# Leaky-ReLU matmul on one core: the first two regions take shorter turns in k, and only the first run of A is turned by TensorE

## The chip, the cores and the metric

One core of a Trainium2 chip runs the kernel. The metric is the device time of one execution in microseconds. Several executions are taken of each kernel, and those of the kernel before are taken on the same chip in the same rounds.

## The reference

```python
def setup_inputs():
    m, k, n = 4096, 4096, 4096
    # a: (m, k) float32 normal, b: (k, n) float32 normal, alpha = 0.01
def reference(a, b, alpha):
    x = np.matmul(a, b)
    return np.where(x > 0, x, alpha * x)
```

## The kernel before

The output is cut into regions of 512 rows by 1024 columns. A region fills all of PSUM: 4 row tiles (`mt`) times 2 column halves (`nt`) are 8 banks. k comes in four units (`u`) of 1024, each of 8 chunks (`c`) of 128. A has to lie with k on the partitions. The usual way there is "strips": GpSimd sends DMAs that cast to bfloat16 and lay four strips of k on four groups of 32 partitions, and VectorE's 32x32 stream transpose (`turn`) does the rest. B comes by casting DMAs of one chunk each.

The first two regions are special, since nothing is there yet. The first unit of A and B comes over the hardware DMA queue as float32 and is cast on chip; A is then transposed by TensorE into PSUM and copied out. The two regions take turns, and what PSUM holds at the end of a turn goes to an SBUF tile `part` (a copy the first time, an add after).

```python
RUNS = [2, 1, 1, 1]                # unit 0 is laid out in two runs of 512 in k
TURNS = [[0], [1], [2, 3]]         # both regions do unit 0, then unit 1, then units 2 and 3
...
order = [("b", 0), ("a", 0, 0, 1), ("a", 1, 0, 1), ("a", 2, 0, 1), ("a", 3, 0, 1)]
order += [("b", 1), ("b", 2), ("a", 0, 1, 2), ("b", 3), ("a", 2, 1, 1), ("a", 3, 1, 1)]
order += [("b", c) for c in range(4, KC)]        # hardware loads, 6 MB in all
...
        if (what, i) == ("b", 3):                # GpSimd's DMAs start behind this copy
            nc.gpsimd.tensor_copy(x[:, :1], b0[:, 3, :1])
...
    turns[1][0](0, 1)                            # transpose the first strips of region 1
    for mt in range(MT):
        spill(0, 0, mt, banks)                   # bank (mt,0) by ScalarE, (mt,1) by VectorE
        if mt == 0:
            turns[1][0](1, 2)
```

## Time and profile before

| what | us | where from |
|---|---|---|
| time, median of 3 | 1783.36 (1783.19 to 1783.38) | runs |
| span of the profiled run | 1781.5 | page |
| lost before and between matmuls | 10.28 | worked out at the top of the prediction |

The one number to watch is the lost time: the end of the last matmul less the 1768.1 us that the matmuls need without a break. I call "stop" a gap between two matmul starts over the normal 216 ns. Some later traces lack 163 of the 8224 matmul records, which shows as single gaps of just two distances (about 432 ns); these are not stops and are left out.

### The profile page before, as it was taken

How to read it: one execution, taken by the hardware profiler on the slowest of the kernel's cores; microseconds unless marked ns; L12 is line 12 of the kernel's file. 1: busy time of each engine (PE TensorE's matmuls, PEld its weight loads, DVE VectorE, ACT ScalarE, POOL GpSimd, SP SyncE). 2: the span in 40 equal slices, each digit the busy share in tenths (PEclk: the TensorE clock that was granted, in tenths of full speed). 3: DMA queues.
4: the chain of work that ended last, by engine and by line, in shares of the span. 5: the costliest groups of instructions: out<-in, count | busy, mean ns of one | idle time of the engine just before them, and what ended most of it. 6: DMA issues, size and time to landing. Idle time of an engine off the chain costs nothing.

```text
span 1781.5 us, 18212 instructions
## 1 busy us (share of the span) xinstructions
PE 1775.6 (100%) x8267; PEld 807.6 (45%) x8267; DVE 144.9 (8%) x123; ACT 152.5 (9%) x271; POOL 366.1 (21%) x667
## 2 busy tenths in 40 slices
PE   9999999999999999999999999999999999999999
PEld 4444444444444444444444444444444444444444
DVE  4530000032000000002200000000220000000000
ACT  2010000000000000000000000000000000000001
POOL 5630200433002020144201202014320110301000
PEclk9999999999999999999999999999999999999999
DMA  9995653988039164398704817449860481835511
GB/s 250 199 251 119 117 128 88 190 130 124 36 95 189 48 121 116 95 192 134 124 24 97 187 48 144 93 105 196 134 122 13 112 172 48 163 73 120 116 48 47
DMA packets 161548, 214.06 MB, mean 120 GB/s; under 512 B 41536, under 2 KB 90816, under 8 KB 161472
## 3 DMA queue, kind: packets, MB, share of 16 engines
q0 software_dynamic: 140608, 139.50, 49.4%
q10 hardware_dynamic: 18432, 67.12, 9.7%
q1 hardware_dynamic: 2432, 6.29, 0.9%
q8 instruction: 64, 1.05, 0.2%
q14 instruction: 12, 0.10, 0.0%
HBM read 285.21 MB, written 67.11 MB: 198 GB/s over the span
## 4 chain that ended last, share of the span: by engine, by line
PE 99%; DMA 0%; ACT 0%; DVE 0%; SPq 0%; issue 0%
PE ps L160 99%; DMA a_in<-in_a_dram 0%; PE turned L290 0%; DVE at L297 0%; ACT at L297 0%; ACT bt L301 0%; DVE a_rounded L273 0%; ACT o L444 0%; SPq L263 0%
## 5 line engine op out<-in xcount | busy, mean ns | idle before, releaser
L160 PE MATMUL ps<-bt,at 128*128 128x512 bf16 x8224 | 1769.8, 378 | 0.5 <-ACT at L297 0.2
L160 PEld LDWEIGHTS <-at 128*128 128x128 bf16 x8224 | 804.2, 98 | 964.1 <-issue 1.4
L140 POOL DMA_DIRECT2D bt<-in_b_dram x408 | 217.1, 538 | 1084.8 <-PE ps L160 1035.8
L429 ACT ACTIVATE o<-ps 128x512 f32<-128x512 f32 x239 | 130.2, 595 | 1518.2 <-PE ps L160 1442.0
L123 DVE STREAM_TRANSPOSE at<-a 128x1024 uint32<-128x1024 uint32 (+2 forms) x64 | 112.5, 1793 | 1154.4 <-DMA a<-in_a_dram 937.9
L117 POOL DMA_DIRECT2D a<-in_a_dram x252 | 148.2, 595 | 194.9 <-DVE at L123 132.4
L238 DVE TENSOR_TENSOR part<-ps,part 128x512 f32<-128x512 f32 x32 | 20.2, 686 | 25.0 <-PE ps L160 25.0
L241 ACT ACTIVATE o<-part 128x1024 f32<-128x1024 f32 x8 | 8.5, 1057 | 77.0 <-DVE part L238 63.4
L301 ACT CAST bt<-b_in 128x512 bf16<-128x512 f32 x8 | 4.9, 619 | 9.6 <-DMA b_in<-in_b_dram 9.6
L234 DVE COPY part<-ps 128x512 f32<-128x512 f32 x8 | 5.3, 681 | 4.0 <-PE ps L160 4.0
L236 ACT COPY part<-ps 128x512 f32<-128x512 f32 x8 | 4.4, 593 | 13.6 <-issue 8.1
L89 PE MATMUL wp<-w 128*128 128x512 bf16 x11 | 4.0, 532 | 1.2 <-DVE x L80 1.2
L290 PE MATMUL turned<-ident,a_rounded 128*128 128x128 bf16 x32 | 2.9, 222 | 1.0 <-DVE a_rounded L273 1.0
L301 DVE CAST bt<-b_in 128x512 bf16<-128x512 f32 x8 | 3.5, 440 | 4.1 <-DMA b_in<-in_b_dram 4.1
L273 DVE CAST a_rounded<-a_in 128x512 bf16<-128x512 f32 (+1 forms) x7 | 3.2, 469 | 5.7 <-DMA a_in<-in_a_dram 5.6
L290 PEld LDWEIGHTS <-a_rounded 128*128 128x128 bf16 x32 | 2.2, 115 | 3.0 <-DVE a_rounded L273 2.7
L89 PEld LDWEIGHTS <-w 128*128 128x128 bf16 x11 | 1.3, 127 | 3.4 <-issue 1.9
L350 POOL CAST x<-bt 128x1 f32<-128x1 bf16 x1 | 0.2, 183 | 12.1 <-ACT bt L301 12.1
L297 ACT COPY at<-turned 128x512 bf16<-128x512 bf16 x4 | 2.3, 586 | 0.7 <-PE turned L290 0.5
L297 DVE COPY at<-turned 128x1024 bf16<-128x1024 bf16 x2 | 1.4, 692 | 1.2 <-PE turned L290 1.2
L86 ACT ACT_TABLE_LOAD x1 | 1.3, 1283 | 1.2 <-PEq L463 1.2
L444 ACT ACTIVATE o<-ps 128x256 f32<-128x256 f32 x2 | 0.8, 384 | 6.0 <-PE ps L160 6.0
(9 smaller groups left out, 1.4 us busy)
## 6 DMA issues: line engine op xcount, KB each, us to landing
bt<-in_b_dram POOLq DMA_DIRECT2D x408, 256.0 KB, 8.0
out_dram<-o ACTq DMA_DIRECT2D x127, 512.0 KB, 3.3
a<-in_a_dram POOLq DMA_DIRECT2D x244, 128.0 KB, 5.3
b_in<-in_b_dram SPq DMA_DIRECT2D x7, 512.0 KB, 8.5
a_in<-in_a_dram SPq DMA_DIRECT2D x6, 256.0 KB, 5.2
b_in<-in_b_dram ACTq DMA_DIRECT2D x1, 512.0 KB, 4.7
a_in<-in_a_dram SPq DMA_DIRECT2D x1, 512.0 KB, 7.6
a<-in_a_dram POOLq DMA_DIRECT2D x8, 64.0 KB, 5.3
```

The costliest lines, as they stand in the source:

```text
L89: nc.tensor.matmul(wp, w[:, :P], w, start=True, stop=True)
L117: nc.gpsimd.dma_start(to, src.rearrange("(g i) w -> i g w", i=32))
L123: nc.vector.transpose(dst.rearrange("p c m e -> p c (m e)").bitcast(U32) .rearrange("p c (g i) -> p g c i", i=32), held[0][:, 4 * t0:4 * t ...
L140: nc.gpsimd.dma_start(new_b(pi, u)[:, c, :], b_rows(n, u, c))
L160: nc.tensor.matmul(ps, plain(t)[:, c, rows] if (mb, h, u) == (0, 0, 0) else t[:, c // 2, rows, c % 2], bt[pi, u][:, c, cols or slice(nt * ...
L234: nc.vector.tensor_copy(kept, banks[mt, nt])
L236: nc.scalar.copy(kept, banks[mt, nt])
L238: nc.vector.tensor_add(kept, banks[mt, nt], kept)
L241: nc.scalar.activation(o, part[h][:, mt, :], LRELU, alpha=alpha)
L290: nc.tensor.transpose(turned[:, c, slot, :], cols[:, i + t, c, :], ident)
L301: copy(b0[:, i, columns(nt)], b_in[i][:, columns(nt)])
L429: nc.scalar.activation(o[:, cols], banks[mt, nt], LRELU, alpha=alpha)
```

## The change

The intent: TensorE's second batch of transposes sits in its stream before 16 us. If region 0 starts with 512 of k only, and region 1 takes over, the second run of A can come as strips instead. It then needs a finer set of turns (512, 512, 512, 1536, 2048, 2048, 1024 of k), and half of the hardware loads move to GpSimd's queue.

```diff
-RUNS = [2, 1, 1, 1]
+SEGS = [(0, 0, 4), (0, 4, 4), (1, 0, 8), (2, 0, 8), (3, 0, 8)]     # unit, first chunk, chunks
-TURNS = [[0], [1], [2, 3]]
+TURNS = [(0, [0]), (1, [0]), (0, [1]), (1, [1, 2]), (0, [2, 3]), (1, [3, 4]), (0, [4])]
+WHERE = {1: [4, 4, 4, 4], 2: [2, 2, 4, 4], 4: [3, 5, 5, 5]}        # where transposes go
...
-order = [("b", 0), ("a", 0, 0, 1), ...                              # 15 hardware loads
+order = [("b", 0)] + [("a", mt) for mt in range(MT)] + [("b", c) for c in range(1, kc0)]   # 8
...
-        if (what, i) == ("b", 3):
-            nc.gpsimd.tensor_copy(x[:, :1], b0[:, 3, :1])
+        if (what, i) == ("a", MT - 1):
+            nc.gpsimd.tensor_copy(x[:, :1], a_rounded[:, i, :1])
...
-        made = pieces_a(0, h, u, i == 1) if i else []
+        made = pieces_a(0, h, s, 2 if i in (1, 3) else None) if i else []
...                                                                  # last two regions:
+                        if r >= len(regions) - 2 and not (final and mt == MT - 1):
+                            nc.scalar.dma_start(to[:, cols], o[:, cols])      # stores by halves
```

In the short turns of region 1 (steps 1 and 3) A's strips come in two pieces of two row tiles, 8 DMAs of 64 KB; step 2, the short turn of region 0, has one piece of four row tiles, 4 DMAs of 128 KB.

More of the change, by code (lines that the diff above doesn't have):

```diff
@@ L60 @@
     KW = KC * P
-    assert TURNS[0] == [0] and sum(TURNS, []) == list(range(KU)) and len(RUNS) == KU
+    assert sum(kc for _, _, kc in SEGS) == KU * KC
+    SEGS_OF = [[s for s in range(len(SEGS)) if SEGS[s][0] == u] for u in range(KU)]
     small_pool = ctx.enter_context(tc.tile_pool(name="small", bufs=1))
@@ L80 @@
     nc.vector.memset(x, 0.0)
-    b_two = [part_pool.tile([P, KC // 2, RN], FP32, name="b_in", tag="part") for _ in range(2)]
-    b_in = [b_two[c // 4][:, c % 4, :] for c in range(KC)]
-    per = KC // RUNS[0]
-    src = b[:per * P, :RN].rearrange("(p c) n -> p c n", p=P)
-    nc.scalar.dma_start(b_in[0], src[:, 0, :])
+    kc0 = SEGS[0][2]
+    kw0 = kc0 * P
+    b_in = part_pool.tile([P, kc0, RN], FP32, name="b_in", tag="part")
+    nc.scalar.dma_start(b_in[:, 0, :], b[:kw0, :RN].rearrange("(p c) n -> p c n", p=P)[:, 0, :])
     nc.scalar.activation(x, x, LRELU, alpha=alpha)
@@ L102, in new_b, with k_of, load_a @@
         return bt[pi, u]
-    def load_a(mb, h, u, mt, tiles, r):
-        kw = KW // RUNS[u]
-        kc = kw // P
-        k0 = u * KW + r * kw
+    def k_of(s):
+        u, c0, kc = SEGS[s]
+        return (u * KC + c0) * P, kc * P
+    def load_a(mb, h, s, mt, tiles):
+        u, c0, kc = SEGS[s]
+        k0, kw = k_of(s)
         row = ((mb * HALVES + h) * MT + mt) * P
@@ L120, in turn @@
         def turn(t0=0, t1=tiles):
-            rows = slice((mt + t0) * P, (mt + t1) * P)
-            dst = new_a(mb, h, u)[:, r * kc // 2:(r + 1) * kc // 2, rows, :]
+            dst = new_a(mb, h, u)[:, c0 // 2:(c0 + kc) // 2, (mt + t0) * P:(mt + t1) * P, :]
             nc.vector.transpose(
@@ L130, in load_a, with b_rows, load_b, pieces_a @@
         return fetch, turn
-    def b_rows(n, u, c):
-        per = KC // RUNS[u]
-        k0 = u * KW + c // per * per * P
-        src = b[k0:k0 + per * P, n * RN:(n + 1) * RN]
-        return src.rearrange("(p c) n -> p c n", p=P)[:, c % per, :]
-    def load_b(pi, n, u, c):
-        nc.gpsimd.dma_start(new_b(pi, u)[:, c, :], b_rows(n, u, c))
-    def pieces_a(mb, h, u, urgent=False):
-        tiles = 2 * RUNS[u]
-        pieces = [load_a(mb, h, u, mt, tiles, r) for mt in range(0, MT, tiles)
-                  for r in range(RUNS[u])]
-        if urgent:
-            pieces[:1] = [load_a(mb, h, u, mt, 2, 0) for mt in range(0, MT, 2)]
-        return pieces
-    def pieces_b(pi, u):
-        return [lambda c=c: load_b(pi, pairs[pi], u, c) for c in range(KC)]
+    def b_rows(n, s, c):
+        k0, kw = k_of(s)
+        src = b[k0:k0 + kw, n * RN:(n + 1) * RN]
+        return src.rearrange("(p c) n -> p c n", p=P)[:, c, :]
+    def load_b(pi, n, s, c):
+        u, c0, _ = SEGS[s]
+        nc.gpsimd.dma_start(new_b(pi, u)[:, c0 + c, :], b_rows(n, s, c))
+    def pieces_a(mb, h, s, tiles=None):
+        tiles = tiles or 2 * KC // SEGS[s][2]
+        return [load_a(mb, h, s, mt, tiles) for mt in range(0, MT, tiles)]
+    def pieces_b(pi, s):
+        return [lambda c=c: load_b(pi, pairs[pi], s, c) for c in range(SEGS[s][2])]
     def plain(t):
@@ L161, in mm @@
             ps,
-            plain(t)[:, c, rows] if (mb, h, u) == (0, 0, 0) else t[:, c // 2, rows, c % 2],
+            plain(t)[:, c, rows] if (mb, h, u) == (0, 0, 0) and c < kc0 else t[:, c // 2, rows, c % 2],
             bt[pi, u][:, c, cols or slice(nt * NT, (nt + 1) * NT)],
@@ L197 @@
             lead = 2 if pi == 1 else KU
-            loads.setdefault(first * KU + u - lead, []).extend(pieces_b(pi, u))
+            for s in SEGS_OF[u]:
+                loads.setdefault(first * KU + u - lead, []).extend(pieces_b(pi, s))
     for mb in range(1, MB):
@@ L203 @@
                 at_slot = first * KU + h * KU + u - 2 * KU + 1
-                for fetch, turn in pieces_a(mb, h, u):
-                    loads.setdefault(at_slot, []).extend([fetch, turn])
+                for s in SEGS_OF[u]:
+                    for fetch, turn in pieces_a(mb, h, s):
+                        loads.setdefault(at_slot, []).extend([fetch, turn])
     def quarter_of(pieces, quarter):
@@ L212, with spill @@
     steps = [
-        (t, h, u, i == 0, i == len(turn) - 1)
-        for t, turn in enumerate(TURNS)
-        for h in range(HALVES)
-        for i, u in enumerate(turn)
+        (h, s, i == 0, i == len(turn) - 1)
+        for h, turn in TURNS
+        for i, s in enumerate(turn)
     ]
+    finals = [max(i for i, step in enumerate(steps) if step[0] == h) for h in range(HALVES)]
     fetches = []
     turns = []
-    for i, (_, h, u, _, _) in enumerate(steps):
-        made = pieces_a(0, h, u, i == 1) if i else []
-        fetches.append([fetch for fetch, _ in made] + (pieces_b(0, u) if i and h == 0 else []))
+    for i, (h, s, _, _) in enumerate(steps):
+        made = pieces_a(0, h, s, 2 if i in (1, 3) else None) if i else []
+        new = i and all(s != before[1] for before in steps[:i])
+        fetches.append([fetch for fetch, _ in made] + (pieces_b(0, s) if new else []))
         turns.append([turn for _, turn in made])
     part = {}
-    def spill(t, h, mt, banks):
+    def spill(i, mt, banks):
+        h = steps[i][0]
+        fresh = all(step[0] != h for step in steps[:i])
         for nt in range(NP):
             kept = part[h][:, mt, nt * NT:(nt + 1) * NT]
-            if t == 0:
-                if nt:
-                    nc.vector.tensor_copy(kept, banks[mt, nt])
-                else:
-                    nc.scalar.copy(kept, banks[mt, nt])
-            else:
-                nc.vector.tensor_add(kept, banks[mt, nt], kept)
-        if t == len(TURNS) - 1:
+            if not fresh:
+                nc.vector.tensor_add(kept, banks[mt, nt], kept)
+            elif nt:
+                nc.vector.tensor_copy(kept, banks[mt, nt])
+            else:
+                nc.scalar.copy(kept, banks[mt, nt])
+        if i == finals[h]:
             o = o_pool.tile([P, RN], FP32, name="o")
@@ L242, in spill @@
             nc.scalar.dma_start(place(0, h, pairs[0], mt), o)
-    runs = RUNS[0]
-    rw = per * P
-    assert runs == 2
-    a_rounded = at_pool.tile([P, MT, KW], BF16, name="a_rounded", tag="at")
-    a_in = bt_pool.tile([P, MT, KW], FP32, name="a_in", tag="bt")
-    order = [("b", 0), ("a", 0, 0, 1), ("a", 1, 0, 1), ("a", 2, 0, 1), ("a", 3, 0, 1)]
-    order += [("b", 1), ("b", 2), ("a", 0, 1, 2), ("b", 3), ("a", 2, 1, 1), ("a", 3, 1, 1)]
-    order += [("b", c) for c in range(4, KC)]
+    a_rounded = at_pool.tile([P, MT, kw0], BF16, name="a_rounded", tag="at")
@@ L255, in columns @@
+    a_in = bt_pool.tile([P, MT, kw0], FP32, name="a_in", tag="bt")
+    order = [("b", 0)] + [("a", mt) for mt in range(MT)] + [("b", c) for c in range(1, kc0)]
     def columns(nt):
         return slice(nt * NT, (nt + 1) * NT)
-    for what, i, *more in order:
+    for what, i in order:
         if what == "a":
-            r, tiles = more
-            k = slice(r * rw, (r + 1) * rw)
-            src = a[i * P:(i + tiles) * P, k].rearrange("(t p) k -> p t k", p=P)
-            nc.sync.dma_start(a_in[:, i:i + tiles, k], src)
+            nc.sync.dma_start(a_in[:, i, :], a[i * P:(i + 1) * P, :kw0])
@@ L264 @@
         elif i:
-            nc.sync.dma_start(b_in[i], b_rows(pairs[0], 0, i))
+            nc.sync.dma_start(b_in[:, i, :], b_rows(pairs[0], 0, i))
     a0 = new_a(0, 0, 0)
     b0 = new_b(0, 0)
-    both = []
-    def round_a(i, r, tiles):
-        k = slice(r * rw, (r + 1) * rw)
-        nc.vector.tensor_copy(a_rounded[:, i:i + tiles, k], a_in[:, i:i + tiles, k])
-    def turn_a(i, r, tiles):
-        k = slice(r * rw, (r + 1) * rw)
-        shared = r and tiles == 1
-        if shared and i == MT - 1:
-            turned = both.pop()
-        else:
-            tag = "ps7" if r else f"ps{4 + i}"
-            turned = psum_pool.tile([P, per, 2 if r else 1, P], BF16, name="turned", tag=tag)
-        if shared and i < MT - 1:
-            both.append(turned)
-        cols = a_rounded[:, :, k].rearrange("m t (p c) -> m t c p", c=per)
-        for t in range(tiles):
-            slot = i - (MT - 2) if shared else t
-            for c in range(per):
-                nc.tensor.transpose(turned[:, c, slot, :], cols[:, i + t, c, :], ident)
-        if both:
-            return
-        first = MT - 2 if shared else i
-        to = plain(a0)[:, r * per:(r + 1) * per, first * P:(i + tiles) * P]
-        turned = turned.rearrange("p c t m -> p c (t m)")
-        copy = nc.vector.tensor_copy if r else nc.scalar.copy
-        copy(to, turned)
@@ L299, in round_b, with round_a, turn_a @@
+    def round_a(i):
+        nc.vector.tensor_copy(a_rounded[:, i, :], a_in[:, i, :])
+    def turn_a(i):
+        turned = psum_pool.tile([P, kc0, P], BF16, name="turned", tag=f"ps{4 + i}")
+        cols = a_rounded[:, i, :].rearrange("m (p c) -> m c p", c=kc0)
+        for c in range(kc0):
+            nc.tensor.transpose(turned[:, c, :], cols[:, c, :], ident)
+        nc.scalar.copy(plain(a0)[:, :kc0, i * P:(i + 1) * P], turned)
     def round_b(i):
         for nt, copy in ((0, nc.scalar.copy), (1, nc.vector.tensor_copy)):
-            copy(b0[:, i, columns(nt)], b_in[i][:, columns(nt)])
+            copy(b0[:, i, columns(nt)], b_in[:, i, columns(nt)])
@@ L305, with work @@
     there = {"a": [], "b": []}
     waiting = []
-    late = []
     banks = {}
-    open_bank = {"late": False}
-    def mm0(mt, c, nt, stop=False):
-        if (mt, nt) == (MT - 1, NP - 1) and not open_bank["late"]:
-            late.append(c)
-            return
-        started = (mt, nt) in banks
-        if not started:
-            banks[mt, nt] = new_bank(mt, nt)
-        mm(banks[mt, nt], 0, 0, 0, 0, mt, nt, c, not started, stop)
-    def work(keep=0):
+    def work(keep=0, stop=False):
@@ L321, in work @@
         now = waiting[:len(waiting) - keep]
         del waiting[:len(now)]
-        for nt in range(NP):
-            for mt, c in now:
-                mm0(mt, c, nt)
-    def ahead(n):
-        return next(m for m in range(len(order) - n) if order[n + 1 + m][0] == "b")
-    round_a(*order[1][1:])
-    for n, (what, i, *more) in enumerate(order):
-        if what == "a":
-            r, tiles = more
-            if n > 1:
-                round_a(i, r, tiles)
-            turn_a(i, r, tiles)
-            work(2 if r and ahead(n) else 0)
-            there["a"] += [(i + t, r) for t in range(tiles)]
-            waiting += [(i + t, c) for t in range(tiles) for c in there["b"] if c // per == r]
+        for mt, c in now:
+            for nt in range(NP):
+                started = (mt, nt) in banks
+                if not started:
+                    banks[mt, nt] = new_bank(mt, nt)
+                mm(banks[mt, nt], 0, 0, 0, 0, mt, nt, c, not started, stop)
@@ L341 @@
+    round_a(0)
+    for n, (what, i) in enumerate(order):
+        if what == "a":
+            if i:
+                round_a(i)
+            turn_a(i)
+            work()
+            waiting += [(i, c) for c in there["b"]]
         else:
@@ L343 @@
             work()
-            there["b"].append(i)
-            waiting += [(mt, i) for mt, r in there["a"] if i // per == r]
-            if n < len(order) - 1:
-                work(2 if ahead(n) else 1)
-        if (what, i) == ("b", 3):
-            nc.gpsimd.tensor_copy(x[:, :1], b0[:, 3, :1])
-        if (what, i) == ("a", MT - 1) and more[0]:
-            open_bank["late"] = True
-            for c in late:
-                mm0(MT - 1, c, NP - 1)
+            waiting += [(mt, i) for mt in there["a"]]
+            if i < kc0 - 1:
+                work(keep=1)
+        there[what].append(i)
+        if (what, i) == ("a", MT - 1):
+            nc.gpsimd.tensor_copy(x[:, :1], a_rounded[:, i, :1])
     part[0] = part_pool.tile([P, MT, RN], FP32, name="part", tag="part")
@@ L357 @@
         fetch()
-    for nt in range(NP):
-        for mt, c in waiting:
-            mm0(mt, c, nt, stop=c == KC - 1)
+    work(stop=True)
     turns[1][0](0, 1)
     for mt in range(MT):
-        spill(0, 0, mt, banks)
+        spill(0, mt, banks)
         if mt == 0:
@@ L366 @@
     turns[1][1]()
-    turns[1][2]()
     for fetch in fetches[2]:
@@ L371 @@
     for i in range(1, len(steps)):
-        t, h, u, first, last = steps[i]
-        head = 0 if h else KC // 2 if last else KC
+        h, s, first, last = steps[i]
+        u, c0, kc = SEGS[s]
+        coming = all(s != step[1] for step in steps[:i])
+        head = 0 if not coming else kc // 2 if last else kc
         groups = [([(mt, c) for c in range(head) for mt in range(MT)], None)]
-        if i == 1:
-            head = KC // RUNS[u]
-            groups = [([(mt, c) for mt in range(MT) for c in range(head)], None)]
-        groups += [([(mt, c) for c in range(head, KC)], mt if last else None) for mt in range(MT)]
-        following = turns[i + 1] if i + 1 < len(steps) else []
-        where = [0, 3]
+        groups += [([(mt, c) for c in range(head, kc)], mt if last else None) for mt in range(MT)]
+        groups += [([], None)]
+        made = turns[i + 1] if i + 1 < len(steps) else []
+        tiles = MT // max(1, len(made))
+        following = [(turn, t) for turn in made for t in range(tiles)]
+        where = WHERE.get(i, [0, 0, 3, 3])
         own = 2 * KU - 2 + i - (len(steps) - 2)
@@ L396 @@
                 for nt in range(NP):
-                    mm(banks[mt, nt], 0, h, 0, u, mt, nt, c, first and c == 0,
-                       last and c == KC - 1)
-            for piece, turn in enumerate(following):
-                if where[piece] == g:
-                    turn()
+                    mm(banks[mt, nt], 0, h, 0, u, mt, nt, c0 + c, first and c == 0,
+                       last and c == kc - 1)
+            for mt, (turn, t) in enumerate(following):
+                if where[mt] == g:
+                    turn(t, t + 1)
             if leaves is not None:
-                spill(t, h, leaves, banks)
+                spill(i, leaves, banks)
     for r in range(HALVES, len(regions)):
@@ L429 @@
                         nc.scalar.activation(o[:, cols], banks[mt, nt], LRELU, alpha=alpha)
-                    if not final or mt < MT - 1:
+                        if r >= len(regions) - 2 and not (final and mt == MT - 1):
+                            nc.scalar.dma_start(to[:, cols], o[:, cols])
+                    if r < len(regions) - 2:
                         nc.scalar.dma_start(to, o)
```

## The prediction

> **What bounds the kernel now.** I read the page first, then the chain of waits, then the start in order of time. Section 1 and the two TensorE groups of section 5:
>
> ```profile
> PE 1775.6 (100%) x8267; PEld 807.6 (45%) x8267; DVE 144.9 (8%) x123; ACT 152.5 (9%) x271; POOL 366.1 (21%) x667
> L160 PE MATMUL ps<-bt,at 128*128 128x512 bf16 x8224 | 1769.8, 378 | 0.5 <-ACT at L297 0.2
> L290 PE MATMUL turned<-ident,a_rounded 128*128 128x128 bf16 x32 | 2.9, 222 | 1.0 <-DVE a_rounded L273 1.0
> ```
>
> TensorE is busy throughout, so only what it does or waits for counts. The 378 ns is the pipelined length of one matmul; the start-to-start distance in the trace, averaged over any 512 matmuls after the first two regions, is 215.83 ns. Of the 8224 matmuls, 8160 have 512 columns and 64 have 256, which is the work of 8192 full ones: 8192 x 0.21583 = 1768.1 us, and the change leaves every one of them. The chain of waits puts the end of the last matmul at 1778.38 us. So the whole cost of starting, stalling and transposing is 1778.38 - 1768.10 = 10.28 us, and behind it there is a tail of 3.1 us (span 1781.5) and 1.9 us outside the span (1783.36). Two per cent would be 35.7 us: that can't be won, since the start, tail and frame together are 15.3 us. The question is how many of the 10.28 us go.
>
> The chain, from the first transposes on (start us, us, what):
>
> ```profile
> 6.63 0.41 PE turned L290 x4
> 7.04 0.46 PE ps L160 x2
> 7.50 0.22 PE turned L290 x4
> 7.72 0.60 PE ps L160 x2
> 8.33 0.24 PE turned L290 x4
> ...
> 9.17 0.53 ACT bt L301
> 9.70 0.04 issue
> 9.74 2.53 PE ps L160 x11
> 12.27 0.60 PE turned L290 x8
> 12.87 1.08 PE ps L160 x5
> ...
> 14.58 0.55 PE turned L290 x8
> 15.13 0.02 issue
> 15.15 0.70 DVE at L297
> 15.85 0.04 issue
> 15.89 1762.46 PE ps L160 x8196
> ```
>
> The reader should see that TensorE hardly runs free until 15.89: two batches of eight transposes (the second k run of the first A block) and a copy out of PSUM stand in its stream. The same stretch on VectorE and GpSimd:
>
> ```profile
> 7.48 0.43 DVE L273 CAST a_rounded<-a_in 128x512 bf16<-128x512 f32 x1 [0.23 <-DMA a_in<-in_a_dram]
> 13.38 0.18 POOL L350 CAST x<-bt 128x1 f32<-128x1 bf16 x1 [12.07 <-ACT bt L301]
> 13.49 5.09 POOL L117 DMA_DIRECT2D a<-in_a_dram  x8
> 20.80 0.45 DVE L123 STREAM_TRANSPOSE at<-a 128x256 uint32<-128x256 uint32 x1 [0.82 <-DMA a<-in_a_dram]
> 23.28 0.69 DVE L234 COPY part<-ps 128x512 f32<-128x512 f32 x1 [2.04 <-PE ps L160]
> 24.25 1.85 DVE L234 COPY part<-ps 128x512 f32<-128x512 f32 x3
> ```
>
> GpSimd is held until 13.38 by a dummy copy that waits for B's fourth chunk, and only then sends for region 1's A. That A is first transposed at 20.80, while TensorE is ready for region 1 at about 23.7: some 2.9 us in hand.
>
> **What the Trainium skill says.** "TensorE: Matmul & The Clock Gate", in "Wait — 56ns, not 53.3ns?", gives back-to-back starts of N / 2.4 GHz + 2.5 ns: 215.7 ns at N = 512 and 55.6 at N = 128. The trace agrees: 215.83 ns, and four transposes in 0.22 us, 55 each. "DMA: Bandwidth & Descriptors", in "SWDGE vs HWDGE vs iDMA", says that a DMA that casts has to come from GpSimd, whose software writes the descriptors, and that the engines share themselves between that queue and the hardware ones. Here GpSimd needs 0.57 to 0.92 us an issue, and those sent at 13.49 landed from 19.87 on, just after the last hardware load (19.53). The same page, "Where 436 GB/s comes from", has a ceiling of 435 GB/s; B's 512 KB chunks land 1.28 us apart in the start, 410 GB/s, so the DMA engines are full there. "PSUM — Partial Sum Buffer", "Specifications (TRN2)", gives 8 banks: a region uses all eight (4 x 2), so each turn's end must empty banks before the next turn may write them; the copies at 23.28 and 24.25 do this.
>
> **The change part by part.**
>
> Removed. (a) Sixteen TensorE transposes, L290 x8 twice: 0.60 + 0.55 = 1.15 us in the chain. (b) Bank (3,1) served these transposes, so its matmuls waited; at 9.74 before has done 7 matmuls, after will have done 8: 0.22 us. (c) Gaps in matmul starts after 9.74 over the normal distance: 0.12 at 11.9 (waiting for the second run), 0.19 at 13.6, 0.30 at 15.4 (the PSUM copy), 0.15 at 23.7 (the bank copy): 0.76. Together 2.13; about 0.14 more lies in short transitions around the transposes, by difference from the next sum.
>
> After's first turn, then: start, first four transposes and B chunks 0 and 1 as before, so chunk 1's matmuls start at 9.74 with 8 done. 24 remain: 9.74 + 24 x 0.21583 = 14.92 us. B's chunks 2 and 3 have no A load between them any more, so they land at 10.04 and 10.04 + 1.28 = 11.32 (before: 12.67). With a 0.62 us cast chunk 3 is ready at about 12.0, wanted at 13.2. No wait. The lost time to there is 14.92 - 32 x 0.21583 = 8.01 us instead of 10.28: **2.27 us is the most that can be won.**
>
> Moved. The GpSimd gate is now A's fourth cast, 7.48 + 0.43 = 7.91, so its DMAs start at about 8.1 instead of 13.49. The fourth, which completes the first two strips of region 1, is issued at about 10.15. Before, the same one took 5.1 us, slowed by the hardware queue; lightly loaded DMAs (the one issued at 20.15) took 3.4. So strips land at 13.5, at worst 15.2. The step order on VectorE is transpose (0.45), bank copy (0.69), transpose. Landing at 13.5: bank (0,1) is free at about 14.65, before the second matmul of the turn at 15.13. Landing at 15.2: the copy ends at 16.3, and TensorE waits some 1.1 us.
>
> Turn 2 (region 0, k 512 to 1024) is due at 14.92 + 6.91 = 21.8 us. Its A is issued until 15.7 and lands at 18.8 to 20.1; its B chunk 0 follows by 1.25 us, at 20.1 to 21.4, the others 1.25 us apart, while TensorE takes 1.73 per chunk. VectorE has 3 copies, four transposes at 0.36 net and one copy: 20.3 to 23.05; TensorE wants the last bank at 23.3. Turn 3 opens at 28.7 with strips that land at 27 to 28.5 in two pieces (the second by 31). The 1536 turn's second part opens at 35.6 and wants B chunk 0, for which 10.5 MB must have come in; before had them at 33.75, by then some 1 MB went by fast hardware loads that now comes as 512-byte pieces, about 0.9 us slower: 34.7 at worst against 35.6.
>
> Added. Seven turn ends instead of six: 8 more VectorE adds of 0.61 us net, 4.9 us beside TensorE; in turn 2 the eight adds and four transposes take 6.3 us of a 6.9 us turn, with about 1 us in hand at each bank. Off the path unless a landing is late. The final stores in halves come out earlier, but the last store is the same SyncE one: tail unchanged.
>
> Sum: 2.27 won, less about 0.4 for waits at the new ends (0.3 at the first, where before has 0.15 in a roomier place, 0.1 elsewhere): 1783.36 - 2.27 + 0.40 = **1781.5 us**.
>
> **The rivals.** (1) All margins hold: no new wait, 1781.1 us. For it: the landings come out earlier than the needs everywhere in the sum, and GpSimd starts 5.4 us earlier. Against: margins of 0.4 to 1 us, each from a chain of estimates. (2) The wait moves to the software DMA: TensorE stands at the first or second turn end until strips land. For it: before's first strips took 6.4 to 7 us from first issue, and the second run now costs GpSimd issues of 0.6 us for pieces that move in 0.42. That costs 1 to 1.5 us: 1782.1 to 1782.6. (3) VectorE becomes the bound in the short turns, as a transpose that waits for a landing stands ahead of a bank copy in its strict order: one late landing then holds both operand and bank. Worth 0.5 to 1 us more: with (2), up to 1783.4, no gain at all. Against: VectorE is idle for most of 8 to 23 us in before, apart from short casts.
>
> **Range and chances.** Waits do not add up: a turn that starts late relaxes the next landings, so the largest lateness counts. The floor is 1781.1 less a little spread (before's three runs span 0.2 us): 1780.9. Rival 2 in full gives the upper end, 1782.7. A gain or loss of 2% is out of reach for the start alone: a loss would need 36 us of waits. Faster 0.005, same 0.985, slower 0.01.
>
> **What would show each step right or wrong.** The chain should have 4 transposes x4, no x8, and matmuls without a break from 9.74; TensorE's turn 0 should end near 14.9; GpSimd's first DMA should issue near 8.1 and VectorE's first stream transpose start near 13.6 to 15.3. B chunk 3 should be cast by 12.1. If the matmul starts show gaps near 15, 22, 28.7 or 35.6 us, their releaser tells which: a DMA of A strips or B chunks is rival 2; a VectorE copy or add is rival 3. The last matmul should end 1.9 us earlier than 1778.38, and the tail stay 3.1 us. The prediction is wrong if the hardware loads are slowed by the earlier software DMAs (chunk 3 later than 13.2), if the strips land after 15.5, or if the tail moves.

## More of the kernel before

Every run in this document is fast (mean granted TensorE clock 0.998 to 1.000), so all can be compared. Stops and landings are read from one profiled run of each kernel.

All DMAs of GpSimd take eight semaphores in turn: each waits until the one eight places before it has landed. So at most eight are in flight.

## The result, and the profile after

| kernel | median us | all runs |
|---|---|---|
| before | 1783.28 | 1783.07 to 1783.60 (6) |
| changed | 1784.73 | 1783.66 to 1786.19 (6) |

The ratio is 1.0008 (95% interval 0.9996 to 1.0021). A ratio is the mean time of one kernel's fast runs over that of the other's of the same rounds, so not quite the ratio of these medians. The time is the same within 2%, as forecast, but 1.4 us up at the median where 1.9 us down was forecast. The spread went from 0.5 to 2.5 us, which is itself a hint: something that varies from run to run now ends TensorE's waits.

The same lines of section 1 and 5 of the changed kernel (1784.35 us, span 1782.6):

```profile
PE 1775.6 (100%) x8251; PEld 807.3 (45%) x8251; DVE 147.1 (8%) x141; ACT 150.3 (8%) x267; POOL 372.5 (21%) x679
L162 PE MATMUL ps<-bt,at 128*128 128x512 bf16 x8224 | 1769.4, 378 | 2.6 <-DMA bt<-in_b_dram 2.5
L273 PE MATMUL turned<-ident,a_rounded 128*128 128x128 bf16 x16 | 2.0, 264 | 0.1
```

The sixteen transposes are gone, as planned. But matmuls now have 2.6 us of idle time, where before they had 0.5, and nearly all of it is ended by B's DMAs. The chain of waits (start us, us, what) says the same:

```profile
8.59 7.35 POOL a L124 x12
15.94 1.63 POOL bt L146 x3
17.57 8.88 DMA bt<-in_b_dram
...
31.33 5.32 DMA a<-in_a_dram
36.65 0.28 issue
36.93 9.96 DMA bt<-in_b_dram
46.89 0.04 issue
46.94 1732.53 PE ps L162 x8058
1779.49 0.38 ACT o L402
```

In the kernel before, TensorE itself carried the chain from 15.89 on. Now the chain up to 46.89 is GpSimd issuing DMAs and DMAs landing; TensorE takes it over only then. Read as in the prediction, at the start of ScalarE's last piece, the last matmul ends at 1779.49, so the lost time is 11.39 us instead of 10.28. The starts of the matmuls show three stops and no other break after 10 us: 0.85 us at 21.7, 1.15 at 36.4, 0.97 at 45.8, together 2.97. Without these the lost time would be 8.42, near the 8.01 of the prediction. The tail is 3.1 us as before.

GpSimd's own timeline in this run (start us, us; an issue of a DMA is what is timed):

```profile
8.01 0.18 POOL L312 CAST x<-a_rounded 128x1 f32<-128x1 bf16 x1 [6.70 <-DVE a_rounded L267]
8.59 7.35 POOL L124 DMA_DIRECT2D a<-in_a_dram  x12 [0.40 <-issue]
15.93 2.18 POOL L146 DMA_DIRECT2D bt<-in_b_dram  x4
18.10 1.75 POOL L124 DMA_DIRECT2D a<-in_a_dram  x3
...
22.95 0.58 POOL L124 DMA_DIRECT2D a<-in_a_dram  x1 [1.65 <-DMA bt<-in_b_dram]
...
26.74 5.17 POOL L124 DMA_DIRECT2D a<-in_a_dram  x9 [0.75 <-DMA bt<-in_b_dram]
```

Two things are to be seen. From 8.59 to about 20 us GpSimd issues without a break: each A DMA costs it about 0.6 us, whether it carries 64 or 128 KB, so the first four chunks of B are sent only from 15.93. Then, to 26.7, it sends one DMA whenever one has landed.

### The profile page after: what moved, and what is told of

Same layout as the page of the kernel before. It is cut to its first block, busy times and chain, and to the rows that moved or that the text cites. A ratio compares the mean times of both kernels' runs of the same rounds, so it can differ in the third digit from the quotient of the medians.

```text
span 1782.6 us, 18214 instructions
## 1 busy us (share of the span) xinstructions
PE 1775.6 (100%) x8251; PEld 807.3 (45%) x8251; DVE 147.1 (8%) x141; ACT 150.3 (8%) x267; POOL 372.5 (21%) x679
## 4 chain that ended last, share of the span: by engine, by line
PE 97%; DMA 2%; POOL 1%; issue 0%; SPq 0%; DVE 0%; ACT 0%; POOLq 0%
PE ps L162 97%; DMA bt<-in_b_dram 1%; POOL a L124 1%; DMA a<-in_a_dram 0%; DMA a_in<-in_a_dram 0%; POOL bt L146 0%; SPq L260 0%; DVE a_rounded L267 0%; ACT o L402 0%; POOL x L312 0%; POOLq L312 0%
## 5 line engine op out<-in xcount | busy, mean ns | idle before, releaser
L124 POOL DMA_DIRECT2D a<-in_a_dram x260 | 152.4, 591 | 200.9 <-DVE at L129 127.2
L240 DVE TENSOR_TENSOR part<-ps,part 128x512 f32<-128x512 f32 x40 | 25.3, 682 | 31.8 <-PE ps L162 31.8
```

The costliest lines, as they stand in the source:

```text
L124: nc.gpsimd.dma_start(to, src.rearrange("(g i) w -> i g w", i=32))
L240: nc.vector.tensor_add(kept, banks[mt, nt], kept)
```

## The experiments

The first theory (L) has two arms: GpSimd's time is fixed per DMA, and only eight are in flight, so DMAs of 64 KB leave the sixteen DMA engines short of work and all that comes behind is late. Its rival (B) says that the engines are simply full and the software queue moves these bytes no faster. Others are named where they come up. Each kernel ran five times, and all results were correct but that of e8. No verdict at 2% is other than "same", so the theories are told apart by the medians with their ranges and, above all, by the landings and stops in the traces. The kernel before had a median of 1783.18 to 1783.31 us beside them in each batch.

The table gathers what the profiled run of each showed. Landing times are read from the DMA completions in the trace, as the last of a DMA's sixteen engines, and are in us from the span's start: of B's first chunk for the second run, of the last strip of turn 3 (region 1's second 512 of k), and of B's first chunk for the 1536 turn. Undisturbed, TensorE would want these at about 21.8, 31 and 35.6. I count turns from 0, as the prediction does. Of the expectations, those of e7 and e9 count from 1 ("third turn" is turn 2), and that of e12 means turn 3.

| run | median us (range) | stops us (at us) | B, 2nd run | strips | B, 1536 |
|---|---|---|---|---|---|
| changed | 1784.73 (1783.66-1786.19) | 0.85 (21.7), 1.15 (36.4), 0.97 (45.8) | 22.67 | 29.41 | 37.73 |
| e0_after | 1784.26 (1783.48-1784.88) | 1.13 (21.9), 1.62 (36.8), 0.63 (46.6) | 23.07 | 29.88 | 38.59 |
| e1_one_piece | 1783.04 (1782.48-1783.20) | 0.89 (28.5), 0.29 (37.6) | 21.45 | 29.00 | 35.68 |
| e2_head6 | 1785.30 (1784.34-1787.57) | 0.74 (21.6), 2.28 (36.2), 1.00 (52.3) | 22.45 | 29.94 | 38.63 |
| e5_half_b | 1784.54 (1784.20-1785.50) | 0.23 (23.7), 1.10 (26.1), 1.87 (36.9), 0.92 (47.0) | 21.91 | 30.08 | 38.92 |
| e4b_gate0 | 1782.81 (1782.70-1784.15) | 0.97 (35.3), 0.58 (44.5) | 21.22 | 28.08 | 36.46 |
| e4_no_gate | 1782.94 (1782.61-1784.94) | 0.55 (35.8), 0.74 (44.6) | 19.38 | 28.14 | 36.56 |
| e3_one_gate0 | 1782.26 (1781.42-1783.48) | 0.45 (28.6), 0.29 (37.3), 0.13 (44.5) | 20.62 | 28.66 | 36.00 |
| e7_hw_b | 1789.46 (1788.52-1790.10) | 4.75 (21.6), then matmuls 0.43 apart to 31.2 | 18.32 | 28.95 | 37.32 |
| e8_half_bytes | 1781.24 (1781.20-1781.37) | none | 20.73 | 26.77 | 34.54 |
| e9_one_all_gate0 | 1782.08 (1781.69-1782.34) | 0.32 (14.8), 0.35 (15.4) | 18.54 | 26.02 | 32.68 |
| e10_one_all | 1782.88 (1782.67-1782.96) | 0.96 (14.8), 0.35 (16.0) | 19.96 | 27.74 | 34.38 |
| e11_copy_first | 1781.77 (1781.62-1782.05) | 0.32 (14.7) | 18.41 | 25.91 | 32.55 |
| e12_one_first | 1782.81 (1782.43-1782.94) | 0.72 (14.8), 0.35 (15.7) | 19.77 | 27.01 | 35.58 |

(In e5 the first chunk is two DMAs, the later of which is given. Stops of under 0.5 us before 10 us, in the first transposes, come in all and are left out.)

### e0_after: the changed kernel again

No edit. 

> The changed kernel again, unedited, as the yardstick of this batch on this chip. Both theories: 1783.7 to 1786.2 us, as in its six runs on record, with three stops of TensorE in the first 50 us (about 0.85, 1.15 and 0.97 us in the profiled run).

It held: 1784.26 us, with the same three stops in other sizes. The stop at 21.9 lies where B's first chunk lands at 23.07, 0.4 us later than in the other profile. The profile puts two of its stops down to VectorE (1.0 us to a bank copy, 1.5 us to a stream transpose). That is a coincidence of times: TensorE went on 0.13 and 0.04 us after B's chunks had landed, as in the profile on record (0.14 and 0.04), and there the same bank copy ended only after TensorE had started again (23.03 against 22.81).

### e1_one_piece: turn 3's strips as four DMAs of 128 KB

```diff
-        made = pieces_a(0, h, s, 2 if i in (1, 3) else None) if i else []
+        made = pieces_a(0, h, s, 2 if i == 1 else None) if i else []
```

> Region 1's strips of the second k run come as 4 DMAs of 128 KB instead of 8 of 64 KB: same bytes, same 512-byte runs. Theory L (GpSimd has only eight DMAs in flight, taken in turn, so small DMAs leave the engines short of work): the strips behind them are issued some 4 us earlier, the stop at 36.4 us goes (1.15 us), the one at 45.8 shrinks to about 0.4: 1.3 to 1.7 us faster than the changed kernel of this batch. Theory B (the DMA engines are full, short runs cost them too much): bytes and runs are the same, so the stops stay: within 0.4 us.

1.2 us faster than e0 at the medians, a little short of L's 1.3 to 1.7 and far from B's 0.4. B's first chunk of the 1536 turn lands 2.9 us earlier with the same bytes in runs of the same length. The stop at 36 us is gone but for 0.29; a new one of 0.89 stands at 28.5, because the whole piece has to land (29.00) before any of it can be transposed. I had not put that into the expectation. The stop at 21.7 is gone too, which this edit can hardly have caused: the first sixteen DMAs are the same, and B's first chunk, the thirteenth, happened to land at 21.45 there. So with the same issues as in the changed kernel it can be 1.2 to 1.6 us earlier; what goes with that is said under what stays open.

### e2_head6: the order of the matmuls in the 1536 turn

```diff
-        head = 0 if not coming else kc // 2 if last else kc
+        head = 0 if not coming else kc * 3 // 4 if i == 4 else kc // 2 if last else kc
```

> In region 1's 1536 turn the chunk-by-chunk part covers 6 of 8 B chunks instead of 4. Both theories on the late strips: the first two stops stay. Theory H (the stop at 45.8 us comes from the order of the matmuls, which wants chunks 4 to 7 all at once): that stop of 0.97 us goes, 0.9 to 1.0 us faster. If the landing of the last chunk is itself the bound whatever the order: no change.

The stop at 45.8 is gone, so it was the order: the turn's second half goes tile by tile and wants four chunks at once. In the changed kernel TensorE starts again at 37.77; 38 matmuls later, at 45.97, it wants the last chunk, which lands at 46.89. But no time was won, 1785.3 us. The stop at 36.2 was longer in the profiled run, and a new one of 1.00 stands at 52.3. VectorE's timeline of this run shows why:

```profile
49.95 2.48 DVE L240 TENSOR_TENSOR part<-ps,part 128x512 f32<-128x512 f32 x4 [10.36 <-PE ps L162]
52.35 1.07 DVE L129 STREAM_TRANSPOSE at<-a 128x512 uint32<-128x512 uint32 x1
```

With the tiles' ends bunched, four adds come in a row, and the transpose that the next turn's first matmul needs stands behind them until 53.4. VectorE's strict order holds TensorE here for 1.0 us, as the third rival feared, but the other way round: adds hold a transpose, no landing is late, and the kernel provokes it.

### e5_half_b: B's four chunks of the second run as eight DMAs

```diff
-        nc.gpsimd.dma_start(new_b(pi, u)[:, c0 + c, :], b_rows(n, s, c))
+        if (pi, s) == (0, 1):
+            for nt in range(NP):
+                cols = slice(nt * NT, (nt + 1) * NT)
+                nc.gpsimd.dma_start(new_b(pi, u)[:, c0 + c, cols], b_rows(n, s, c)[:, cols])
+            return
+        nc.gpsimd.dma_start(...)
```

> The four B chunks of the second run come as 8 DMAs of 128 KB instead of 4 of 256 KB: the number of DMAs goes up, bytes stay, runs halve from 4 to 2 KB. Theory L: four more places of the eight are taken, later issues slip by some 2 to 4 us, the stops at 36.4 and 45.8 grow: 1 to 3 us slower. Theory B: runs of 2 KB are still long, so within 0.5 us.

A miss for L's number: 1784.54 against 1784.26 us, inside the spread. The last of the four chunks lands at 27.34 instead of 26.86, and the 1536 turn's first at 38.92 instead of 38.59. So more DMAs cost little where the queue ahead of them is long and GpSimd waits for landings anyway. Either theory can live with this run; doubling the count there was a poor test.

### e4b_gate0 and e4_no_gate: when GpSimd starts

```diff
-        if (what, i) == ("a", MT - 1):
+        if (what, i) == ("a", 0):                       # e4b: gate at A's first cast
             nc.gpsimd.tensor_copy(x[:, :1], a_rounded[:, i, :1])
```

In e4_no_gate the copy is left out altogether. 

> GpSimd's first DMA waits for A's first cast (about 5.7 us) instead of its fourth (7.9), so the software queue starts about 2 us earlier. Theory S (all landings are late because that queue is served late and slowly, so its whole schedule moves with its start): the strips and B chunks come about 2 us earlier, the stops at 21.7 and 36.4 go (2.0 to 2.7 us), the one at 45.8 shrinks; the hardware loads lose perhaps 0.3 us: 1781.3 to 1782.6. Theory C (while the hardware queue is busy the software queue gets hardly anything): landings move by under 0.5 us, time 1783.5 to 1785.

> No gate at all: GpSimd issues from about 1 us. Theory S: as with the early gate or better for the later stops, but now the first hardware loads share the engines with eight strips (1 MB): the first matmul starts 0.3 to 2 us later; total 1781.5 to 1783.5. Theory C: first matmul late by under 0.3 us, stops as they were, 1783.5 to 1785.

Both gain about 1.4 us over the changed kernel (1782.81 and 1782.94), so the start of the software queue matters, as S said. But S's sizes were too good: 1782.81 lies in neither range, 1782.94 in S's. GpSimd's first DMA went out 2.4 us earlier in e4b (6.21) than in the changed kernel (8.59), yet the strips of turn 3 and the 1536 turn's B landed only 1.3 us earlier, and 0.97 and 0.58 of stops stayed. With no gate the first DMA went out at 1.33, and the landings at 28 and 36.5 are those of e4b; the hardware loads were slowed by about 1.1 us (B's fourth chunk landed at 12.84, in e4b at 11.78), though the first matmul, at 7.09, was no later than in other runs (6.77 to 7.17). Starting earlier still only lets eight DMAs wait in line.

### e3_one_gate0: both edits

The edits of e1 and e4b together. 

> The early gate and the one-piece strips together. If both work on the same lateness (landings against needs), the sum is capped by the floor: no stops left, or one of under 0.5 us at the turn that opens at 28.5; 1781.1 to 1782.0, under both kernels. If the early gate does nothing, as the one-piece kernel: 1782.5 to 1783.2.

1782.26 us, under both as said at the median, but outside 1781.1 to 1782.0, and with one run above: five runs from 1781.42 to 1783.48. Small stops at 28.6, 37.3 and 44.5 are still landings against needs.

### e7_hw_b: the second run's B over the hardware queue

```diff
-        new = i and all(s != before[1] for before in steps[:i])
+        new = i > 2 and all(s != before[1] for before in steps[:i])      # GpSimd leaves this B out
...
+    staged = bt_pool.tile([P, kc0, RN], FP32, name="staged", tag="bt")
+    nc.vector.memset(staged[:, :, :1], 0.0)              # holds the loads until strips have landed
+    for c in range(kc0):
+        nc.sync.dma_start(staged[:, c, :], b_rows(pairs[0], 1, c))
...                                                       # casts by ScalarE and VectorE in step 1
```

> The second run's B comes over the hardware queue as float32, issued after the first strips have landed, and is cast by ScalarE and VectorE; GpSimd keeps only A and the later B. Theory L (eight in flight): four long DMAs leave the eight places, strips of the fourth turn and everything behind come 4 to 6 us earlier, stops at 36.4 and 45.8 go; at 21.8 a stop of 0 to 1.2 us, as the strips of the third turn now share with a busy hardware queue: 1781.2 to 1782.6. Theory B (the engines are simply full): the bytes are the same, landings of the 1536 turn move by under 1 us and its stops stay: 1783.5 to 1785.

5 us slower, and neither theory said so. B itself came early (18.32). But turn 2's strips, sent at the same time, landed from 21.26 to 25.94, where the changed kernel had them by 20.44. TensorE waited 4.75 us for the transpose of these strips, and it came back slow. Two stretches of this run (us; PE, PEld, DVE, ACT, POOL busy with counts, mean granted clock, DMA share, GB/s):

```profile
20.00:28.00 8.00, 3.41 (x14) 1.27 (x12) 2.96 (x8) 2.83 (x5) 3.44 (x7) 0.77 1.37 204
28.00:36.00 8.00, 8.00 (x32) 3.26 (x30) 3.69 (x9) 0.00 (x0) 7.22 (x14) 0.80 1.27 166
```

The 0.77 and 0.80 are means over the stretches: by the trace's clock record the grant was 0.50 from 24.35 to 31.18 us, and the matmuls in that time start 0.43 us apart instead of 0.216. So 32 were done in 8 us where the changed kernel did 39. The Trainium skill, "TensorE: Matmul & The Clock Gate", "Part 1: The HAM clock gate", has the array go back to half its clock after at least one idle window of about 3.4 us. The half agrees with this run. The time doesn't: the record has the clock fall 2.5 us after the last matmul before the stop began (21.82). The stops of up to 2.28 us elsewhere left the clock at 1.00. The 1536 turn's B landed at 37.32, hardly before the 37.73 of the changed kernel: B's forecast of this landing was right and L's of 4 to 6 us wrong, since the strips ahead had been held up by the hardware queue. The same skill's "DMA: Bandwidth & Descriptors", "Queues, rings and completion order", says that an engine takes turns between its queues packet by packet. The trace lists a strip in pieces of 256 bytes and B's float32 rows in pieces of 4 KB. If each piece were such a packet, turns would give the strips little, and the run agrees with that; but it shows neither the turns nor that a piece is a packet in the page's sense, so this cause is not shown.

### e8_half_bytes: less to land (wrong result)

Only the left half of B's columns is loaded for the second run and the first unit after it, and the matmuls of both halves read it. All instructions stay; 3 MB less come in.

```diff
-        nc.gpsimd.dma_start(new_b(pi, u)[:, c0 + c, :], b_rows(n, s, c))
+        half = slice(0, NT) if (pi, s) in ((0, 1), (0, 2)) else slice(0, RN)
+        nc.gpsimd.dma_start(new_b(pi, u)[:, c0 + c, half], b_rows(n, s, c)[:, half])
```

> Wrong result on purpose: of B's chunks for the second run and the 1536 turn only the left 512 columns are loaded, and both column halves of the matmuls read them; every matmul, bank copy, add and DMA count stays, 3 MB less have to come in. If the stops are all lateness of landings: the two at 36.4 and 45.8 go and the one at 21.7 goes or shrinks under 0.4, and the kernel reaches the 1781.1 us that the prediction called the most that can be won, within 0.4. If turn ends or VectorE's order (rival 3) hold TensorE too: stops remain, 1782 or more. If the floor itself is wrong, matmuls run without stops and the time is still over 1781.6.

No stop at all after the first transposes, 1781.24 us, and five runs within 0.17 us. The result is wrong (relative error 0.14), as it must be. This splits the prediction in two: what it said of TensorE, of VectorE in the short turns, of the turn ends and of the floor (1781.1) holds; what fails is when the data land.

### e9_one_all_gate0, e10_one_all and e12_one_first: which strips make it late

```diff
-        made = pieces_a(0, h, s, 2 if i in (1, 3) else None) if i else []
+        made = pieces_a(0, h, s, None) if i else []           # e12: 2 if i == 3 else None
...
-    turns[1][1]()
+    turns[1][0](2, 4)
```

e9 has the early gate of e4b besides, e10 and e12 the late one of the change. 

> The early gate, and the strips of both short turns of region 1 in one piece each (4 DMAs of 128 KB, not 8 of 64): eight fewer DMAs ahead of the 1536 turn. Theory L: GpSimd no longer waits at 10.5 to 12.4 us for a place among eight, the third turn's strips are issued some 3 us earlier, all stops but a small one at turn 1 (up to 0.4) go: 1781.2 to 1782.0 and less spread. Theory B: nothing over the one-piece kernel with the early gate, 1781.9 to 1782.6.

> As the one before but with the gate where the change has it (A's fourth cast): tells the two edits apart. Turn 1 now waits for all four strips of one piece: about 0.3 to 1 us at 14.9. Theory L: later stops under 0.5 in sum, so 1781.8 to 1782.8. Theory B: as the one-piece kernel with the late gate plus the new stop, 1783 to 1784.

> Late gate as in the change; only the first short turn's strips in one piece, the third turn's as 8 DMAs of 64 KB. If GpSimd's time per issue at the start made everything late: B's first software chunk lands near 20 us as in the run with both, the stop at 21.7 goes, the one at turn 1 is about 1.3 in sum, those at 36 and 46 stay under 0.6 in sum: 1782.8 to 1783.4. If it was the third turn's pieces that held the eight places: stops at 36 and 46 stay at 1 us or more: 1783.8 to 1784.8. Slow packets of 2 KB near 19 to 21 us: none if they come with the first 64 KB strips.

With both short turns' strips in one piece (e10) every stop after the first turn is gone, and the spread with them: 1782.67 to 1782.96. The 1536 turn's B lands at 34.38, 3.3 us earlier than in the changed kernel with the same bytes, in runs of the same length. The times alone would not have decided it: e10's 1782.88 lies just outside both ranges, and e9's 1782.08 in B's, 0.08 us above L's. The landing does: it is earlier than in any run of the changed kernel with 64 KB pieces, and that is the end of theory B. Three stretches of the changed kernel (columns as above):

```profile
12.00:20.00 8.00, 8.00 (x38) 3.63 (x37) 5.03 (x10) 3.42 (x7) 7.85 (x14) 1.00 1.32 125
20.00:28.00 8.00, 7.32 (x35) 3.18 (x34) 3.42 (x8) 1.17 (x2) 3.52 (x7) 1.00 1.25 172
28.00:36.00 8.00, 8.00 (x39) 3.60 (x38) 7.45 (x13) 0.00 (x0) 7.15 (x13) 1.00 1.26 152
```

and of e10:

```profile
12.00:20.00 8.00, 6.97 (x31) 2.95 (x31) 4.35 (x9) 2.88 (x7) 6.81 (x12) 1.00 1.42 166
20.00:28.00 8.00, 7.95 (x38) 3.64 (x38) 3.67 (x8) 1.53 (x3) 4.03 (x7) 1.00 1.46 192
28.00:36.00 8.00, 8.00 (x38) 3.62 (x38) 8.00 (x15) 0.00 (x0) 5.63 (x11) 1.00 1.24 194
```

The last column counts bytes as they are written, in bfloat16: 125, 172 and 152 GB/s became 166, 192 and 194. So the engines of the changed kernel moved less than they could.

e12 tells what the first short turn's pieces cost. With only these strips in one piece the stops at 21.7, 36 and 46 are gone as well (1782.81), and turn 3's strips land at 27.01 instead of 29.41. That doesn't clear turn 3's pieces. From the last of turn 3's strips to B's first chunk of the 1536 turn the same bytes come in, and by the table that takes 8.3 to 8.8 us in the eight kernels with 64 KB pieces in turn 3 (the changed one, e0, e2, e5, e4b, e4, e7, e12), but 6.6 to 7.3 us in the five with one piece (e1, e3, e9, e10, e11; e8 loads fewer bytes). So each of the two counts. Either edit alone leaves 1.1 to 1.2 us of stops instead of 3.0 to 3.4, in e1 with the help of the early landing. GpSimd's timeline in e12:

```profile
8.48 5.27 POOL L124 DMA_DIRECT2D a<-in_a_dram  x8 [0.40 <-issue]
13.75 2.19 POOL L146 DMA_DIRECT2D bt<-in_b_dram  x4
```

Eight strip DMAs instead of twelve come ahead of B, which is issued at 13.75 instead of 15.93: four issues saved, 2.1 us of GpSimd's time in all. B's first chunk lands at 19.77 instead of 22.67. The price is the stop at turn 1, 1.07 us in two parts, as all four row tiles must now land before the first can be transposed. The early gate of e9 brings that down to 0.67.

### e11_copy_first: VectorE's order at the first turn's end

```diff
-    turns[1][0](0, 1)
     for mt in range(MT):
         spill(0, mt, banks)
-        if mt == 0:
-            turns[1][0](1, 2)
+        if mt < 2:
+            turns[1][0](mt, mt + 1)
```

on top of e9. 

> Early gate and one-piece strips in both turns, and VectorE now copies bank (0,1) out before the first stream transpose, not after it. Theory V (a transpose that waits for a landing holds a bank copy that could have gone ahead): of the two stops at 14.8 (0.32) and 15.4 us (0.35) the second goes: 1781.7, 0.3 to 0.4 faster than without. Otherwise no change, 1782.1.

What TensorE waited for after 10 us in e9, then in e11 (engine, tile and line waited for: us in all, times, longest):

```profile
PE ps L162 <- DVE part L242: 0.2, 1, 0.2
PE ps L162 <- DVE at L129: 0.2, 1, 0.2
```

```profile
PE ps L162 <- DVE at L129: 0.2, 1, 0.2
```

The wait for the bank copy is gone, the stop of 0.35 with it, and 0.3 us of time at the medians: 1781.77 us, as forecast (the ranges of e9 and e11, from two batches, overlap, so the trace shows this and the time only agrees). All five runs (1781.62 to 1782.05) lie under all nine of the kernel before beside it (1783.05 to 1783.36), 1.4 us by the medians; the ratio is 0.9992, with an interval (0.9980 to 1.0005) that is wider than these spreads and still holds 1. It gives the right result, and beats both kernels by a hair: 0.08% of the kernel before, 2.5 to 3 us of the changed one.

## Why the prediction was wrong

**TensorE's part was right.** The transposes went, matmuls ran unbroken from 9.9 us to the first stop, and turn 0 ended 0.14 us later than the 14.92 worked out: that run's first matmul started at 7.17 instead of 6.89 us, as the granted clock reached 1.00 only at 7.04 us (before: 4.12) and all its warm-up matmuls started 0.43 us apart. e8 shows what is left when nothing is late: 1781.24 us, against the 1781.1 called the most that can be won. The small rest is a slip in the sum: the 10.28 runs to the end of the last matmul, the 8.01 counts distances between starts, and a matmul's end comes 0.16 us later than that (379 less 215.83 ns). The "about 0.14 more" found by difference is this, not time to win; the 2.13 us added up part by part gives 1781.23.

**The first landing was right.** The fourth DMA was to land at 13.5 and did at 13.61; the first stream transpose started at 13.73; no stop at turn 1. The nearness is partly luck: it was issued at 10.57 instead of 10.15 and took 3.04 us instead of the 3.4 borrowed from a DMA of twice the size.

**The step that failed is the sum of landings behind it.** It stood as "Its A is issued until 15.7 and lands at 18.8 to 20.1; its B chunk 0 follows by 1.25 us, at 20.1 to 21.4", and then "about 0.9 us slower: 34.7 at worst against 35.6". Issue ended at 15.94 and A landed at 20.44, little off; but B's chunk 0 came at 22.67, and the 1536 turn's at 37.73, 3.0 us behind the worst case. I had taken the landing distances of the kernel before (1.25 us a chunk, 0.66 us a wide strip), which it reaches with a long queue ahead of the engines. The changed kernel doesn't have that queue. Its first issues carry 64 KB each at 0.6 us of GpSimd's time: that was even noted in the second rival ("GpSimd issues of 0.6 us for pieces that move in 0.42"; the 0.42 has no source there, and in the changed kernel's queue 64 KB strips land 0.36 us apart) but never carried on into the landings. e10 has larger pieces, the same bytes, and lands the 1536 turn's B at 34.38, inside the worst case that I had given.

**A term was left out.** The third stop, 0.97 us at 45.8, has no step in the prediction. "TensorE takes 1.73 per chunk" holds in the first half of the 1536 turn only; in the second half four chunks are wanted within 1.3 us, while they land 1.25 us apart. e2 took this stop away by the order alone.

**The rivals.** The second was the right one and was put at 1 to 1.5 us; it measured 3.0 to 3.4 us of stops in two profiles, at three places instead of one. "Waits do not add up" was the reason for the small size. It fails here because the landings kept falling behind the needs: after the first stop the next need was 0.85 us later, and the landings were 3.0 us later than planned. The third rival was not at work in the changed kernel's two profiles (e0 has the reasons); in its own form, a transpose that waits for a landing ahead of a bank copy, it shows at 0.35 us in e9, e10 and e12, and e11 takes it away.

**What stays open.** Part of the lateness at 21.7 us is in single slow packets, described below; why they are slow no run tells. In the four runs with the same first sixteen DMAs the first B chunk took longer from issue to landing the longer the slowest 2 KB packet was: 5.46 us in e1 (0.96 us), 6.31 in e2 (1.35), 6.74 in the changed kernel (1.63), 6.88 in e0 (2.14). At e1's 21.45, as good as the prediction's worst case of 21.4, there was no stop. So the time per issue alone doesn't account for the first stop, and the spread between runs may come from these packets; that is an order of four, not a proof. And the two arms of theory L (time per issue, eight in flight) were not varied one at a time: e12 saves four issues and frees four places at once.

## What to carry to other kernels

When loads move to a queue whose issue has a fixed price, work out the landings from the count of DMAs and the issuing engine's time as well as from the bytes, and don't borrow distances between landings from a kernel that keeps the queue full. A stop removed in front returns behind as soon as the data are later than TensorE, so give each need its own margin, in the order in which the matmuls want the chunks. A run with half the bytes and a wrong result tells in one go whether landings are what holds the engine.

## What the Trainium skill lacked or had wrong

- "DMA: Bandwidth & Descriptors", "Anatomy of one DMA — SWDGE (gpsimd) path", calls the generation of descriptors a small, variable part of the fixed cost. In these runs an issue holds GpSimd for 0.54 to 0.81 us (three issues took 0.90 to 1.04), about the same for 64, 128 and 256 KB, so 64 KB pieces can't exceed about 115 GB/s (an estimate: 64 KB by 0.57 us). The first eight strips of the changed kernel went out at 109 GB/s (512 KB from 8.59 to 13.40 us).
- The same page, "Queues, rings and completion order", has the taking of turns by packet but not what it does to a queue of small packets: beside a busy hardware queue, a strip DMA issued at 13.43 landed at 21.26 in e7, against 17.38 for the one issued at 13.40 in the changed kernel.
- No page that I found tells of single slow packets like these: in the first 52 us of the changed kernel 22 packets of the software queue took over 0.5 us, up to 1.63, where the usual ones take 0.04 to 0.17; the kernel before has 4. Eight of them are 2 KB packets between 18.9 and 21.5 us, around B's late first chunk. The same stretch (17.9 to 21.6 us) has seven or eight in each of e0, e1, e2, e3, e4b and e4, and four of 1 KB in e5, but none in e9, e10, e11 and e12, whose first strips come as 128 KB DMAs. The cause is open.
- "TensorE: Matmul & The Clock Gate", "Part 1: The HAM clock gate", has the clock fall "after ≥1 idle window (~3.4µs)". By the clock records here it can fall sooner: in e7's stop 2.5 us after the last matmul had begun, and at the end of the program 2.1 to 5.0 us after the last matmul's end in the fourteen traces that record it (under 3.4 us in seven of them).
